# Attention weights transposed in two steps, copies of values moved forward in the queues, and a third raw buffer in the last stage

## The chip, the cores and the metric

The program runs on one core of a Trainium2 chip. The core has four engines that matter here. TensorE (PE in the profile; PEld is its loading of the stationary operand) multiplies matrices into PSUM. VectorE (DVE) and ScalarE (ACT) do element work and move results out of PSUM. SyncE (SP) issues the DMAs. Each engine works through its own queue in order and waits where an instruction needs a result of another engine. The metric is the device time of one execution in microseconds. Three runs of the kernel before took 2829.89, 2833.97 and 2838.74 us; the median is 2833.97.

## The reference, cut to what matters

Two layers work on 512 tokens of width 2048, all in float32. The first is an mLSTM with 8 heads, the second an attention over chunks with 16 heads of width 128; the attention's keys and values come from the residual stream after the first layer. Each layer normalises, modulates with a learned shift and scale, mixes, gates with SiLU, projects back, normalises again and adds to the stream.

```python
def mlstm_mixer(h, w_in, conv_w, conv_b, gate_b, g_head, w_out):
    proj = h @ w_in
    qk = silu(causal_conv(proj[..., :A_V0], conv_w, conv_b))
    v, o, z = ...                       # three more column ranges of proj
    ht = mlstm_chunkwise(q, k, v, li, lf)
    ht = rmsnorm(ht, g_head)
    y = sigmoid(o) * ht * silu(z)
    return y @ w_out

kv = hkv @ kv_w                         # keys and values, shared
qz = h @ w_in                           # queries and gate of the attention
s = einsum('blhd,bkhd->bhlk', q, k) * scale + bias
p = softmax(where(visible, s, -inf))
y = einsum('bhlk,bkhd->blhd', p, v) * silu(z)
x = x + gate * rmsnorm(y @ w_out, g_post)
```

A chunk of 64 queries sees itself and the eight chunks before it, which at 512 tokens is every earlier chunk.

## The kernel before, in words

Float32 products are made of three matmuls each: every operand is split into a high part `hi` (rounded by a copy on ACT, line 181) and a rest `lo` (a subtraction on DVE, line 182), and `mm3` adds `hi*hi`, `hi*lo` and `lo*hi` in PSUM. `split` is this pair, one ACT and one DVE instruction.

Weights come in pieces of 128 x 1024 numbers, 512 KB, in the order in which `stream()` lists them. `wpiece` (line 187) loads a piece into a `raw` buffer, may form sums of its blocks (lines 206 to 208, for products done with seven in place of eight block products, `proj_s`), and splits it into `wh` and `wl` (sums into `wsh` and `wsl`). There are two `raw` buffers (`RAW_BUFS`), and three each of `wh` and `wl`. Where `spare[0]` names a pool, every third piece (`i % 3 == 0`, line 197) takes a `raw` buffer of that pool, so that there are three.

PSUM has eight banks. Five belong to the pool `psP` and hold the products of projections (`newp`); three belong to `psA` and hold all smaller results (`newa`): scores, transposes, the attention's output.

The order of the instructions is not written out by hand. A planner takes them in the order of the program as priority and gives each engine, whenever it is free in the plan, the ready instruction of the highest priority. `tc.high_priority(AHEAD)` makes the instructions in its block count as if they stood 300 instructions earlier (`AHEAD = 300`, line 33). From the second stage on the pieces of weights are prepared under it, and so is the evacuation at the end of `proj_s`.

The stages follow each other:

- The start makes the modulation and the first products. Then eight mLSTM heads (loop at line 619). A head projects its values with `proj_b` into four banks `pv` (line 666), 128 tokens each; the last block of weights finishes the four banks one after the other. Lines 672 to 679 move the four banks to `v` tiles, three of them with `split`, the fourth with a copy. Behind that come the products of the gates: from head `HALF = 4` on `pair` and `proj_s`, which take four banks at once, named d, c, a and b (`ps_dzo`, `ps_czo`, `ps_azo`, `ps_bzo`). In head 4, `head_sums` also makes the sums of the input (`h1s`) on ACT and DVE while the values are projected.
- The output projection of the mLSTM (`rows`), then `values` (line 870): products into banks `ps_kv`, copied to SBUF by ACT at line 880 and stored. `input_sums` makes sums for the keys at the same time. The keys follow with `proj_s` (banks `ps_dk`, `ps_ck`, `ps_ak`, `ps_bk`).
- The attention (lines 973 to 1058). For head `h`, `queries` runs `proj_s` with four pieces of weights; `mid` is called ahead of the third piece. `mid` runs `mixed` for head `h-2` (weights times values into `ps_o`) and `weights` for head `h-1` (scores into `ps_s`, softmax). Behind the projection stands `flipped(h-1)`: ten 128 x 128 transposes into four tiles `ps_t`, for the blocks j = 0 to 3 with 4, 3, 2 and 1 transposes; each tile is evacuated into `pt0` to `pt3`, the first three with `split`; then `vt`, the values of the head, is split into `vv`.
- The output projection (line 1093): four groups `g` of 512 columns. Groups 0 to 2 take all four blocks of tokens at a time; group 3 takes them in two passes of two, the last with three pieces held back (`late=3`), while `finish` normalises and stores the finished rows (line 1091).

## Time and profile before

| | us |
|---|---|
| median of three runs | 2833.97 |
| the profiled execution | 2835.62 |
| its span, first to last instruction | 2833.6 |
| TensorE busy | 2788.1 |
| DVE busy | 2057.1 |
| ACT busy | 1333.3 |

The span is what the profile shows; the 2.0 us between it and the time of the same execution lie outside it. The stages in the span, read from the timeline: mLSTM heads to about 1545 us, their output projection to 1888, values and keys to 2245 (keys from 1981 to 2144), attention to 2654, the last projection to the end.

Rows of the timeline read: start, duration, engine, line, operation, `out<-in` by the program's names, shape, count, and in brackets the idle time before it with what ended it. Rows of the chain read: start, duration, what. Rows of windows give the length, then busy time (and instructions) of PE, PEld, DVE, ACT and POOL, the granted clock of TensorE as a share of full speed, the DMA engines' busy share, and GB/s. Matmuls overlap: the time one takes in a stream is the distance between starts, not its printed duration. Loads of weights appear as `wr<-in_wst`; the page gives a median of 3.5 us from issue to landing for the pieces of 512 KB.

### The profile page before, as it was taken

How to read it: one execution, taken by the hardware profiler on the slowest of the kernel's cores; microseconds unless marked ns; L12 is line 12 of the kernel's file. 1: busy time of each engine (PE TensorE's matmuls, PEld its weight loads, DVE VectorE, ACT ScalarE, POOL GpSimd, SP SyncE). 2: the span in 40 equal slices, each digit the busy share in tenths (PEclk: the TensorE clock that was granted, in tenths of full speed). 3: DMA queues.
4: the chain of work that ended last, by engine and by line, in shares of the span. 5: the costliest groups of instructions: out<-in, count | busy, mean ns of one | idle time of the engine just before them, and what ended most of it. 6: DMA issues, size and time to landing. Idle time of an engine off the chain costs nothing.

```text
span 2833.6 us, 40474 instructions
## 1 busy us (share of the span) xinstructions
PE 2788.1 (98%) x15308; PEld 2421.5 (85%) x15308; DVE 2057.1 (73%) x3488; ACT 1333.3 (47%) x1957; POOL 0.2 (0%) x4
## 2 busy tenths in 40 slices
PE   7999999999999999999999999999999999999998
PEld 5787888888888989989888888888998899999886
DVE  7986978878688776857767445567885788888525
ACT  4234524334234544544545444468434566666523
POOL 0000000000000000000000000000000000000000
PEclk9999999999999999999999999999999999999999
DMA  8875687868764232322324656788435433333624
GB/s 296 298 254 180 229 312 238 300 236 279 265 237 144 103 108 97 109 93 105 108 90 140 217 197 222 244 273 281 171 127 182 163 120 125 129 122 118 221 102 167
DMA packets 177115, 524.59 MB, mean 185 GB/s; under 512 B 18788, under 2 KB 36228, under 8 KB 176408
## 3 DMA queue, kind: packets, MB, share of 16 engines
q1 hardware_dynamic: 176920, 522.01, 54.0%
q8 instruction: 120, 1.97, 0.3%
q14 instruction: 75, 0.61, 0.1%
HBM read 488.33 MB, written 38.85 MB: 186 GB/s over the span
## 4 chain that ended last, share of the span: by engine, by line
PE 85%; DVE 7%; DMA 4%; ACT 2%; issue 2%; SPq 0%; DVEq 0%; ACTq 0%
PE ps_y L223 16%; PE ps_v L223 10%; PE ps_o L223 6%; PE ps_z L223 5%; PE ps_azo L223 4%; PE ps_qk L223 4%; PE ps_kv L223 4%; PE ps_bzo L223 3%; PE ps_l L223 3%; PE ps_az L223 3%; PE ps_cz L223 2%; PE ps_dz L223 2%; PE ps_s L223 2%; PE ps_czo L223 2%; PE ps_dzo L223 2%; DVE wl L182 2%
## 5 line engine op out<-in xcount | busy, mean ns | idle before, releaser
L181 ACT CAST wh<-wr 128x1024 fp32r<-128x1024 f32 (+3 forms) x586 | 585.0, 999 | 824.9 <-PE ps_y L223 201.5
L182 DVE TENSOR_TENSOR wl<-wr,wh 128x1024 fp32r<-128x1024 f32 (+3 forms) x586 | 678.4, 1159 | 396.2 <-ACT wh L181 395.0
L223 PE MATMUL ps_y<-wh,y 128*128 128x512 f32 x1536 | 477.4, 391 | 2.3 <-ACT wh L181 2.3
L223 PEld LDWEIGHTS ps_y<-wh,y 128*128 128x128 f32 x1536 | 288.8, 188 | 63.2 <-ACT wh L181 2.8
L223 PE MATMUL ps_v<-wh,h 128*128 128x512 f32 x1024 | 321.3, 390 | 0.0
L223 PE MATMUL ps_y<-wl,y 128*128 128x512 f32 x768 | 299.8, 390 | 0.3 <-DVE wl L182 0.3
L181 ACT CAST wsh<-ws 128x384 fp32r<-128x384 f32 (+1 forms) x205 | 129.5, 632 | 360.1 <-issue 128.9
L182 DVE TENSOR_TENSOR wsl<-ws,wsh 128x384 fp32r<-128x384 f32 (+1 forms) x205 | 144.3, 704 | 130.2 <-ACT wsh L181 129.7
L223 PEld LDWEIGHTS ps_v<-wh,h 128*128 128x128 f32 x1024 | 192.3, 188 | 39.7 <-issue 0.4
L223 PE MATMUL ps_v<-wl,h 128*128 128x512 f32 x512 | 199.8, 390 | 0.0
L381 DVE CUSTOM_DVE_ANT_0 ada<-ada,scB,cl 128x1024 f32<-128x1024 f32 x128 | 163.7, 1280 | 27.2 <-DMA ada<-in_adaT 26.9
L381 DVE CUSTOM_DVE_ANT_0 ada<-ada,scB,mod 128x1024 f32<-128x1024 f32 x128 | 163.9, 1280 | 23.7 <-DMA ada<-in_adaT 22.1
L223 PEld LDWEIGHTS ps_y<-wl,y 128*128 128x128 f32 x768 | 144.6, 188 | 30.8 <-DVE wl L182 1.1
L223 PE MATMUL ps_kv<-wh,hkv 128*128 128x512 f32 x512 | 159.4, 391 | 0.0
L206 DVE TENSOR_TENSOR ws<-wr 128x256 f32<-128x256 f32 (+1 forms) x205 | 104.8, 520 | 35.7 <-DMA wr<-in_wst 34.3
L223 PE MATMUL ps_qk<-h,wh 128*128 128x512 f32 x384 | 119.1, 390 | 0.0
L223 PE MATMUL ps_o<-h,wh 128*128 128x512 f32 x384 | 118.3, 389 | 0.0
L223 PE MATMUL ps_z<-h,wh 128*128 128x512 f32 x384 | 118.3, 389 | 0.0
L223 PEld LDWEIGHTS ps_v<-wl,h 128*128 128x128 f32 x512 | 96.2, 188 | 19.7 <-issue 0.9
L223 PEld LDWEIGHTS ps_kv<-wh,hkv 128*128 128x128 f32 x512 | 95.7, 188 | 19.6
L223 PE MATMUL ps_l<-h,wh 128*128 128x512 f32 x320 | 99.6, 393 | 1.0 <-ACT q L467 0.5
L223 PE MATMUL ps_kv<-wl,hkv 128*128 128x512 f32 x256 | 99.8, 390 | 0.0
(385 smaller groups left out, 5880.8 us busy)
## 6 DMA issues: line engine op xcount, KB each, us to landing
wr<-in_wst SPq DMA_DIRECT2D x520, 512.0 KB, 3.5
ada<-in_adaT SPq DMA_DIRECT2D x256, 512.0 KB, 5.9
xt<-nsc SPq DMA_DIRECT2D x46, 256.0 KB, 3.9
yr<-ysc SPq DMA_DIRECT2D x16, 512.0 KB, 4.4
wr<-in_wst SPq DMA_DIRECT2D x30, 256.0 KB, 4.6
wr<-in_wst SPq DMA_DIRECT2D x16, 384.0 KB, 6.0
bsc<-in_ext SPq DMA_DIRECT2D x16, 320.0 KB, 6.4
xt<-in_xT SPq DMA_DIRECT2D x4, 1024.0 KB, 6.9
```

The costliest lines, as they stand in the source:

```text
L181: nc.scalar.copy(hi, src)
L182: nc.vector.tensor_tensor(lo, src, hi.bitcast(F32), op=ALU.subtract)
L206: nc.vector.tensor_tensor(t[:, : 2 * w], r[:, w : 3 * w], r[:, : 2 * w], op=ALU.subtract)
L223: nc.tensor.matmul(ps, a, b, start=start, stop=stop)
L381: pin(nc.vector.tensor_tensor_reduce(at, at, scB[:, j * D // 2 : (j + 1) * D // 2], 1.0, mod[:, i : i + 1] if j else col(CB + i), ALU.mult ...
```

## The change

Four edits. Lines 672 to 679 move `v` out of PSUM under `high_priority(AHEAD)`, and so does the copy at line 880. In the attention, `flipped` takes the list of its blocks: blocks 0 and 1 stay behind the projection of head `h`, blocks 2 and 3 and the split of `vt` (now `split_v`) move into `turn`, which `queries` of the next head calls ahead of its second piece of weights; `mid` stays ahead of the third. In the last stage, from group 1 on, `spare[0]` is the pool `op`, so every third piece has a `raw` buffer there, 4 KB a partition more.

```diff
         for m in range(4):
-            if m < 3:
-                t = hp.tile([P, 2, S], F32R, tag="qk", name=f"v{h}_{m}", bufs=4)
-                split(t[:, 0, :], t[:, 1, :], pv[m])
-            else:
-                t = hp.tile([P, S], F32, tag="v3", name=f"v{h}_{m}")
-                nc.scalar.copy(t, pv[m])
+            with tc.high_priority(AHEAD):
+                if m < 3:
+                    t = hp.tile([P, 2, S], F32R, tag="qk", name=f"v{h}_{m}", bufs=4)
+                    split(t[:, 0, :], t[:, 1, :], pv[m])
+                else:
+                    t = hp.tile([P, S], F32, tag="v3", name=f"v{h}_{m}")
+                    nc.scalar.copy(t, pv[m])
             v.append(t)
...
-            nc.scalar.copy(v, p)
+            with tc.high_priority(AHEAD):
+                nc.scalar.copy(v, p)
...
-    def queries(h, mid):
+    def queries(h, steps):
...
-        proj_s("b_w_in", ..., kq, (2, 2), {2: mid}, True)
+        proj_s("b_w_in", ..., kq, (2, 2), steps, True)
...
-    def flipped(h, pr):
+    def flipped(h, pr, js):
         pts = []
-        for j in range(4):
+        for j in js:
...
+        return pts
+
+    def split_v(h):
         v = at.tile([P, 2, 384], F32R, tag="vv", name=f"vv{h}")
         split(v[:, 0, :], v[:, 1, :], vt[h][:, :384])
-        return pts, v
+        return v
...
     for h in range(BH + 2):
-        pr = []
+
+        def turn():
+            if h > 1:
+                pts[h - 2] += flipped(h - 2, prs.pop(h - 2), (2, 3))
+                vs[h - 2] = split_v(h - 2)
 
         def mid():
             if h > 1:
-                mixed(h - 2, *ptv.pop(h - 2), szs.pop(h - 2))
+                mixed(h - 2, pts.pop(h - 2), vs.pop(h - 2), szs.pop(h - 2))
             if 0 < h <= BH:
-                pr.extend(weights(h - 1, *qs.pop(h - 1)))
+                prs[h - 1] = weights(h - 1, *qs.pop(h - 1))
...
         if h < BH:
-            qs[h], szs[h] = queries(h, mid)
+            qs[h], szs[h] = queries(h, {1: turn, 2: mid})
         else:
+            turn()
             mid()
         if 0 < h <= BH:
-            ptv[h - 1] = flipped(h - 1, pr)
+            pts[h - 1] = flipped(h - 1, prs[h - 1], (0, 1))
...
     for g in range(4):
+        if g:
+            spare[0] = op
         gate_row(1, g)
```

More of the change, by code (lines that the diff above doesn't have):

```diff
@@ L971, in hybrid_trunk @@
     fetch_k(0)
-    def queries(h, mid):
+    def queries(h, steps):
         z = at.tile([P, 4, 256], F32, tag="z", name=f"z{h}", bufs=2)
-        proj_s("b_w_in", h2, h2s, ATT_PAIRS, z[:, 0:2, :], z[:, 2:4, :], f"z{h}", kq, (2, 2), {2: mid}, True)
+        proj_s("b_w_in", h2, h2s, ATT_PAIRS, z[:, 0:2, :], z[:, 2:4, :], f"z{h}", kq, (2, 2), steps, True)
         qz = z.rearrange("p a t -> p (a t)")
@@ L1037, in mixed @@
         nc.sync.dma_start(y2c[h // 2][:, h % 2, :], sz)
-    qs, ptv, szs = {}, {}, {}
+    qs, pts, prs, vs, szs = {}, {}, {}, {}, {}
     for h in range(BH + 2):
-        pr = []
+        def turn():
+            if h > 1:
+                pts[h - 2] += flipped(h - 2, prs.pop(h - 2), (2, 3))
+                vs[h - 2] = split_v(h - 2)
         def mid():
             if h > 1:
-                mixed(h - 2, *ptv.pop(h - 2), szs.pop(h - 2))
+                mixed(h - 2, pts.pop(h - 2), vs.pop(h - 2), szs.pop(h - 2))
             if 0 < h <= BH:
-                pr.extend(weights(h - 1, *qs.pop(h - 1)))
+                prs[h - 1] = weights(h - 1, *qs.pop(h - 1))
             if h < BH - 1:
```

## The prediction

> **What bounds the kernel now.** I read the page first (busy time, then the chain that ended last), then who TensorE waited for, then the timeline around each of those waits.

> ```profile
> span 2833.6 us, 40474 instructions
> PE 2788.1 (98%) x15308; PEld 2421.5 (85%) x15308; DVE 2057.1 (73%) x3488; ACT 1333.3 (47%) x1957; POOL 0.2 (0%) x4
> ...
> PE 85%; DVE 7%; DMA 4%; ACT 2%; issue 2%; SPq 0%; DVEq 0%; ACTq 0%
> ```

> TensorE is busy for 2788.1 of 2833.6 us and carries 85% of the chain. The change removes no matmul, so it can win only the 45.5 us in which TensorE stands still, and what a standstill costs behind it. The waits of TensorE, as far as the edits touch them:

> ```profile
> PE ps_czo L223 <- DVE v L182: 3.0, 1, 3.0
> PE ps_t L1018 <- DVE pt L182: 2.7, 5, 1.1
> PE ps_y L223 <- ACT wh L181: 2.3, 1, 2.3
> ...
> PE ps_azo L223 <- DVE v L182: 1.0, 1, 1.0
> PE ps_bk L223 <- ACT v L880: 1.0, 1, 1.0
> PE ps_ak L223 <- DVE zk L317: 1.0, 1, 1.0
> ```

> The columns are total us, times and longest. Four places: copies of `v` in one mLSTM head (3.0 + 1.0), a copy of `v` at the end of the values (1.0), the transposes of attention (2.7), the last stage (2.3). The start-up has more, but nothing there is edited.

> **Copies of v in the mLSTM heads (lines 672 to 679).** No instruction is added; the copy on ACT and the subtraction on DVE only move forward in the queues. The `ps_czo` wait occurs once, in head 4, so the other heads get nothing. There:

> ```profile
> 894.10 0.39 PE L223 MATMUL ps_v<-wh,h 128*128 128x512 f32 x1
> 894.28 0.62 ACT L181 CAST h1s<-h1r 128x512 fp32r<-128x512 f32 x1 [0.99 <-DVE h1r L328]
> 894.80 0.58 ACT L181 CAST v<-ps_v 128x512 fp32r<-128x512 f32 x1
> 897.44 0.68 DVE L182 TENSOR_TENSOR v<-ps_v,v 128x512 fp32r<-128x512 f32 x1
> 898.17 0.50 PE L223 MATMUL ps_czo<-h1s,wsh 128*128 128x256 f32 x2 [2.98 <-DVE v L182]
> 900.15 0.79 PE L223 MATMUL ps_azo<-h,wh 128*128 128x256 f32 x2 [1.00 <-DVE v L182]
> ```

> ```profile
> 521.47 43.52 PE ps_o L223 x192
> ```

> A 512-wide matmul takes 43.52/192 = 0.227 us. The last block of the value projection finishes its four banks one after the other, six matmuls each, so the first bank was complete 18 x 0.227 = 4.1 us before 894.3, at about 890.2; its copy began at 894.80, behind casts of `p`, `wh` and `h1s`. Put in front, copy and subtraction take 0.58 + 0.68 = 1.3 us behind whatever runs, so two banks are free before 895.0, where TensorE now stops, and the third about 895. That removes 2.98 + 1.00 = 4.0 us. The clock is given back too:

> ```profile
> 898.00:901.00 3.00, 1.83 (x10) 1.63 (x11) 3.00 (x7) 2.41 (x4) 0.00 (x0) 0.83 0.02 7
> 901.00:904.00 3.00, 3.00 (x11) 2.53 (x11) 2.87 (x7) 0.51 (x1) 0.00 (x0) 0.60 0.50 175
> ```

> The column before the last two is the granted clock: 0.17 x 1.83 + 0.40 x 3.0 = 1.5 us lost. Together -5.5. What is pushed back: three subtractions (2.0 us) go ahead of `h1s` and `p` work on a DVE that is busy for 3.00 of 3.00 us here. If that arrives at the weights' `wl`, 2.0 come back: -3.5 is the poor end. I take -5.5: the row below shows that the next casts of weights wait for TensorE, so they move with it.

> ```profile
> 905.62 1.05 ACT L181 CAST wh<-wr 128x1024 fp32r<-128x1024 f32 x1 [3.49 <-PE ps_bzo L223]
> ```

> [...]

> **Copies of values (line 880).** Again no new instruction.

> ```profile
> 1982.59 0.51 ACT L181 CAST wsh<-ws 128x384 fp32r<-128x384 f32 x1 [1.06 <-DVE ws L208]
> 1983.01 0.58 ACT L880 COPY v<-ps_kv 128x512 f32<-128x512 f32 x1
> ```

> ```profile
> 2001.73 0.41 DVE L314 TENSOR_TENSOR zk<-zk,ps_dk 128x256 f32<-128x256 f32 x1
> 2003.66 0.41 DVE L317 TENSOR_TENSOR zk<-zk,ps_ck 128x256 f32<-128x256 f32 x1
> ```

> The copy stood behind a `wsh` cast that waited 1.06 us on DVE. In front of it, `ps_bk` no longer waits: -1.0. But the next product stops 20 us later on `zk` of line 317, from a DVE that runs without a gap from 2001.73 to there and is not fed by this copy. TensorE would come 1.0 earlier and wait 2.0 in place of 1.0. I take 0, with ends -1.0 and +1.2 (two copies of 0.58 ahead of a `wh`).

> **Transposes in two steps (lines 1012 to 1058).** Ten transposes a head before and after, the same four evacuations, the same split of `vt`. Blocks 0 and 1 (seven transposes) stay behind the head's projection; blocks 2 and 3 (two and one) come behind the first piece of the next one, and so does the split of `vt`.

> ```profile
> 2428.35 1.14 PE L1018 MATMUL ps_t<-kcs,s 128*128 128x128 f32 x9
> 2429.25 0.48 PE L223 MATMUL ps_dz<-h2s,wh 128*128 128x256 f32 x2
> ...
> 2434.58 0.40 PE L223 MATMUL ps_dz<-h2s,wh 128*128 128x256 f32 x2
> 2434.82 0.28 PE L223 MATMUL ps_dz<-h2s,wl 128*128 128x256 f32 x1
> 2434.94 0.28 PE L223 MATMUL ps_dz<-h2s,wh 128*128 128x256 f32 x1
> 2435.29 0.30 PE L1018 MATMUL ps_t<-kcs,s 128*128 128x128 f32 x1
> ```

> ```profile
> 2434.46 1.14 DVE L182 TENSOR_TENSOR pt<-ps_t,pt 128x512 fp32r<-128x512 f32 x2
> ```

> Now nine transposes go at once into three banks, and the tenth waits for the first bank, which DVE frees at about 2435.0. From 2434.94 to 2435.29 are 0.35 us where 256-wide matmuls follow each other every 0.12 (2434.82 to 2434.94): 0.23 lost. Sixteen heads make 3.7, the five longer waits of 2.7 add some 2.3 more, the rest of them being in the 0.23: about 6.0 in all. But the tenth transpose already stands behind the first piece: 2434.58 begins the second one. After the edit it needs the same bank, freed by the same subtraction, whose inputs do not move; it should stand at the same place. And block 2 becomes a group of its own: after the nine, the first pair of matmuls took 0.48 where such a pair takes 0.40, so a third group costs 16 x 0.08 = +1.3. I take +1.0. Ends: -6.0 if the tenth's wait goes, and 16 x (0.23 + 0.08) = +5.0 if block 2 gets such a wait too. The later evacuations are covered by this room:

> ```profile
> 2411.71 0.41 DVE L182 TENSOR_TENSOR pt<-ps_t,pt 128x256 fp32r<-128x256 f32 x1
> ...
> 2414.72 0.96 DVE L182 TENSOR_TENSOR wsl<-ws,wsh 128x768 fp32r<-128x768 f32 x1 [2.40 <-ACT wsh L181]
> ```

> ```profile
> 2414.49 1.73 PE L223 MATMUL ps_o<-pt,vv 128*128 128x512 f32 x9
> ```

> `pt2` is done 2.4 us before `mixed` starts and DVE then idles for 2.4.

> [...]

> **Third raw buffer (line 1093).** From the second of four groups on, every third piece of weights is loaded into a buffer of its own, so a load waits for the piece three back and not two.

> ```profile
> 2805.83 6.61 DMA wr<-in_wst
> ...
> 2812.55 1.05 ACT wh L181
> ...
> 2813.62 1.24 DVE wl L182
> ...
> 2814.91 7.97 PE ps_y L223 x27
> ```

> ```profile
> 2814.00:2817.00 3.00, 2.70 (x8) 1.88 (x7) 1.63 (x2) 1.04 (x1) 0.00 (x0) 0.64 0.23 87
> 2817.00:2820.00 3.00, 3.00 (x12) 2.40 (x12) 0.45 (x1) 0.00 (x0) 0.00 (x0) 0.79 0.00 0
> ```

> In the last pass a piece is 12 matmuls, 2.7 us. The load issued at 2805.83 landed after 6.61 us beside the stores of finished rows; TensorE waited 2.3 for its `wh`, then lost 0.36 x 2.70 + 0.21 x 3.0 = 1.6 at the lower clock. A load issued one piece earlier, 2.7 us, covers the 2.3. I take 2.3 + 1.6 + 0.3 (the stop at 2814.91 on `wl`) = -4.2. Poor end -2.0, if the issue stays behind the stores on SP's queue.

> **Sum.** -5.5 + 0 + 1.0 - 4.2 = -8.7. The profiled execution took 2835.62 us, 2.0 outside its span; it would take 2826.9. It lies 1.65 above the median shown, 2833.97; on that scale the forecast is 2825.3, say 2825. About 0.3%, 8.5 us, is what a measurement of this kernel can tell from no change.

> **Rivals.**
> - The split does what its words say: the bank is free when blocks 2 and 3 come, and the 6.0 of waits go. For it: five of the waits are DVE being late by up to 1.1 us, which a later transpose would not see. Against it: the place of the tenth transpose, above. -5.5 - 6.0 + 1.3 - 4.2 = -14.4: 2819.5.
> - One of the two large gains fails: DVE in head 4 passes its work on to `wl` and the loads stay behind the stores, -3.5 + 1.0 - 2.0 = -4.5: 2829.5.
> - Slower: `pt2` or the split of `vt` falls behind `wsl` and `wl`. From 2414.72 that is 0.96 + 1.24 + 0.41, to 2417.3, where `mixed` wants `pt2` some 1.2 us after 2414.49. A wait of 1.5 us in 16 heads is +24, net +15: 2849. It turns the sign from 0.54 us a head (8.7/16) and means slower by 0.3% from 1.1. Against it: 2.4 us of room on both engines' rows.

> **How the numbers follow.** The forecast's case 40%, its own range 2822 to 2828, split 22 to 18 between faster and within 0.3%; the first rival 33%, faster; the second 13%, within; the slower one 14%. So faster 0.56, within 0.3% 0.30, slower 0.14. The range leaves out the slower case and little else: from 2815 (the first rival with the best ends) to 2836 (the second with block 2's +5.0).

> **What would show it.** Right: no wait of `ps_czo` or `ps_azo` on `v`, a clock of 1.00 from 898 to 904; no wait of `ps_y` on `wh` at the end; the wait of `ps_bk` gone and that of `ps_ak` longer; transposes in three groups a head, with the last still losing 0.2. Wrong: transposes two and three together without a gap; or `ps_o` waiting for `pt` or `vv` in every head.

## The result and the profile after

The changed kernel takes 2824.33 us (median of 7 runs, 2822.36 to 2826.60); the kernel before, run beside it, 2835.13 us (7 runs). The ratio is 0.9962, with a 95% interval from 0.9950 to 0.9974: 10.8 us less (7 to 14), or 0.38%: a little more than the 0.3% that can be told from no change. The forecast was 2825. The profiled execution took 2822.55 us with a span of 2820.4, so it is 1.8 us quicker than the median; 2835.62 was the one before. A difference of two single profiles, 13.1 us here, is therefore good to some 2 us.

The page of the changed kernel, its span, its engines and the shares of the chain:

```profile
span 2820.4 us, 40468 instructions
PE 2784.8 (99%) x15308; PEld 2420.6 (86%) x15308; DVE 2059.4 (73%) x3488; ACT 1332.4 (47%) x1956; POOL 0.2 (0%) x4
...
PE 86%; DVE 6%; DMA 4%; ACT 2%; issue 2%; SPq 0%; DVEq 0%; ACTq 0%
```

TensorE still has the same 15308 matmuls. It stands still for 35.6 us in place of 45.5, and its busy time falls by 3.3, about the 1.5 + 1.6 of clock in the forecast. What it waits for (total us, times, longest):

```profile
PE ps_t L1020 <- DVE pt L182: 2.5, 4, 0.9
...
PE ps_kv L223 <- DVE wl L182: 0.8, 1, 0.8
...
PE ps_ak L223 <- DVE zk L317: 0.7, 1, 0.7
...
PE ps_azo L223 <- DVE v L182: 0.5, 1, 0.5
...
PE ps_czo L223 <- DVE v L182: 0.3, 1, 0.3
```

The wait in head 4 of the mLSTM is down from 3.98 to 0.76, `ps_bk` no longer waits, `ps_y` no longer waits for weights at the end. The transposes wait as they did (2.5 after 2.7). `ps_kv` on `wl`, 0.8, is new.

Head 4 in the timeline of the changed kernel (start, duration, engine, line), and the windows behind it (the granted clock is the third number from the end):

```profile
892.18 1.22 DVE L182 TENSOR_TENSOR wl<-wr,wh 128x1024 fp32r<-128x1024 f32 x1
892.30 0.62 ACT L181 CAST h1s<-h1r 128x512 fp32r<-128x512 f32 x1 [0.96 <-DVE h1r L328]
892.82 0.58 ACT L181 CAST v<-ps_v 128x512 fp32r<-128x512 f32 x1
...
893.52 0.68 DVE L182 TENSOR_TENSOR v<-ps_v,v 128x512 fp32r<-128x512 f32 x1
...
894.26 0.50 PE L223 MATMUL ps_czo<-h1s,wsh 128*128 128x256 f32 x2 [0.26 <-DVE v L182]
```

```profile
898.00:901.00 3.00, 3.00 (x16) 2.49 (x16) 3.00 (x8) 1.13 (x4) 0.00 (x0) 1.00 0.15 40
901.00:904.00 3.00, 3.00 (x21) 2.73 (x20) 3.00 (x7) 1.58 (x3) 0.00 (x0) 1.00 0.38 141
```

The subtraction of `v` comes 0.7 us behind its cast, where it came 2.6 us behind it before (894.80 and 897.44), and the clock stays whole. The cast itself is still behind `h1s`, and the subtraction behind a `wl`: these are the 0.76 that are left. With two or four times the lead (`2 * AHEAD`, `4 * AHEAD`) the planner gives the very same order, so more precedence of this kind has nothing more to give.

The transposes of a head in attention:

```profile
2403.26 0.38 PE L1020 MATMUL ps_t<-kcs,s 128*128 128x128 f32 x2
...
2403.83 0.28 PE L223 MATMUL ps_dz<-h2s,wh 128*128 128x256 f32 x1
2404.18 0.30 PE L1020 MATMUL ps_t<-kcs,s 128*128 128x128 f32 x1
```

Three groups, of seven, two and one. The tenth starts 0.35 us behind a 256-wide matmul, as before: 0.23 lost. The last pass of the last stage:

```profile
2799.00:2802.00 3.00, 3.00 (x15) 2.50 (x14) 3.00 (x5) 1.06 (x1) 0.00 (x0) 1.00 0.90 303
2802.00:2805.00 3.00, 3.00 (x15) 2.49 (x14) 2.49 (x3) 1.05 (x1) 0.00 (x0) 1.00 0.97 371
```

TensorE is busy for all of it at a clock of 1.00, while the DMA engines are 0.90 and 0.97 busy.

### The profile page after: what moved, and what is told of

Its sections match the earlier page's. It is cut to its first block, busy times and chain, and to the rows that moved or that the text cites. A ratio compares the mean times of both kernels' runs of the same rounds, so it can differ in the third digit from the quotient of the medians.

```text
span 2820.4 us, 40468 instructions
## 1 busy us (share of the span) xinstructions
PE 2784.8 (99%) x15308; PEld 2420.6 (86%) x15308; DVE 2059.4 (73%) x3488; ACT 1332.4 (47%) x1956; POOL 0.2 (0%) x4
## 4 chain that ended last, share of the span: by engine, by line
PE 86%; DVE 6%; DMA 4%; ACT 2%; issue 2%; SPq 0%; DVEq 0%; ACTq 0%
PE ps_y L223 17%; PE ps_v L223 10%; PE ps_o L223 5%; PE ps_z L223 5%; PE ps_azo L223 4%; PE ps_qk L223 4%; PE ps_bzo L223 3%; PE ps_kv L223 3%; PE ps_az L223 3%; PE ps_l L223 3%; PE ps_cz L223 3%; PE ps_dz L223 2%; PE ps_s L223 2%; PE ps_czo L223 2%; PE ps_dzo L223 2%; PE ps_bz L223 2%
## 5 line engine op out<-in xcount | busy, mean ns | idle before, releaser
L182 DVE TENSOR_TENSOR wl<-wr,wh 128x1024 fp32r<-128x1024 f32 (+3 forms) x586 | 678.9, 1160 | 397.9 <-ACT wh L181 396.9
L181 ACT CAST wh<-wr 128x1024 fp32r<-128x1024 f32 (+3 forms) x586 | 585.6, 1000 | 802.5 <-PE ps_y L223 216.1
L223 PE MATMUL ps_y<-wh,y 128*128 128x512 f32 x1536 | 476.1, 390 | 0.0
L223 PEld LDWEIGHTS ps_y<-wh,y 128*128 128x128 f32 x1536 | 288.2, 188 | 59.8
L223 PE MATMUL ps_v<-wh,h 128*128 128x512 f32 x1024 | 322.6, 390 | 0.3 <-DVE cv L529 0.2
L223 PE MATMUL ps_y<-wl,y 128*128 128x512 f32 x768 | 299.0, 389 | 0.0
L181 ACT CAST wsh<-ws 128x384 fp32r<-128x384 f32 (+1 forms) x205 | 129.5, 632 | 356.5 <-issue 132.4
L182 DVE TENSOR_TENSOR wsl<-ws,wsh 128x384 fp32r<-128x384 f32 (+1 forms) x205 | 144.4, 704 | 125.0 <-ACT wsh L181 124.6
L223 PEld LDWEIGHTS ps_v<-wh,h 128*128 128x128 f32 x1024 | 192.3, 188 | 40.8 <-issue 1.5
L223 PE MATMUL ps_v<-wl,h 128*128 128x512 f32 x512 | 199.7, 390 | 0.0
L381 DVE CUSTOM_DVE_ANT_0 ada<-ada,scB,mod 128x1024 f32<-128x1024 f32 x128 | 163.9, 1281 | 19.8 <-DMA ada<-in_adaT 18.3
L223 PEld LDWEIGHTS ps_y<-wl,y 128*128 128x128 f32 x768 | 144.2, 188 | 29.2
L223 PE MATMUL ps_kv<-wh,hkv 128*128 128x512 f32 x512 | 159.6, 391 | 0.0
L223 PE MATMUL ps_qk<-h,wh 128*128 128x512 f32 x384 | 119.1, 390 | 0.0
L223 PE MATMUL ps_o<-h,wh 128*128 128x512 f32 x384 | 118.4, 389 | 0.0
L223 PE MATMUL ps_z<-h,wh 128*128 128x512 f32 x384 | 118.2, 389 | 0.0
L223 PEld LDWEIGHTS ps_v<-wl,h 128*128 128x128 f32 x512 | 96.1, 188 | 19.9 <-issue 0.9
L223 PEld LDWEIGHTS ps_kv<-wh,hkv 128*128 128x128 f32 x512 | 95.9, 188 | 19.6
L223 PE MATMUL ps_kv<-wl,hkv 128*128 128x512 f32 x256 | 99.8, 390 | 0.8 <-DVE wl L182 0.8
L223 PE MATMUL ps_l<-h,wh 128*128 128x512 f32 x320 | 99.2, 391 | 1.2 <-ACT oz L467 0.8
```

What stands on the lines that cost most here:

```text
L181: nc.scalar.copy(hi, src)
L182: nc.vector.tensor_tensor(lo, src, hi.bitcast(F32), op=ALU.subtract)
L223: nc.tensor.matmul(ps, a, b, start=start, stop=stop)
L381: pin(nc.vector.tensor_tensor_reduce(at, at, scB[:, j * D // 2 : (j + 1) * D // 2], 1.0, mod[:, i : i + 1] if j else col(CB + i), ALU.mult ...
```

## The experiments

The theory: each part acts in its own place, as the terms of the sum say. The main rival: the two steps of the transposes are where the gain is. The kernel before, run beside each set of experiments, took 2836.2, 2836.3 and 2836.32 us (medians of 26, 10 and 9 runs). Differences below are of medians; intervals are 95%, of the ratio on record. That ratio is not the quotient of the medians and can lie up to 0.001 from it (0.9971 against 0.9979 in the first run, 0.9998 against 1.0008 in the second), so a difference here is good to 2 or 3 us.

**One part at a time.** First the copies of `v` in the mLSTM heads alone:

```diff
-            if m < 3:
+            with tc.high_priority(AHEAD):
+                if m < 3:
...
```

> Only the copies of v in the mLSTM heads take precedence. Theory (the parts add, each in its own place): the profile of the changed kernel still shows ps_azo waiting 0.50 and ps_czo 0.26 in head 4, and the clock whole there; so 4.0 - 0.76 of wait and about 1.2 of clock go: -4.4 us against the kernel before (-5.5 as forecast, -3.5 at the poor end), a ratio near 0.9984, and no wait elsewhere grows. Rival (DVE passes its work on to the weights): -2 or less, with a wait on wl or wh behind head 4.

Measured 2830.22 us, -6.0, ratio 0.9971 (0.9960 to 0.9981). The waits of TensorE from 880 to 2144 us:

```profile
PE ps_ak L223 <- DVE zk L317: 0.6, 1, 0.6
PE ps_azo L223 <- DVE v L182: 0.5, 1, 0.5
...
PE ps_czo L223 <- DVE v L182: 0.3, 1, 0.3
```

Head 4 is as in the changed kernel. Another 1.4 us of waits are gone 1100 us later, in a stage that this edit does not touch: `ps_bk` does not wait for the copy of values, and `ps_ak` waits 0.6 in place of 1.0. The rows at that place, of the kernel before and then of this one, show what the copy no longer stands behind:

```profile
1981.66 0.69 DVE L206 TENSOR_TENSOR ws<-wr 128x512 f32<-128x512 f32 x1 [1.26 <-DMA wr<-in_wst]
```

```profile
1976.04 0.68 DVE L206 TENSOR_TENSOR ws<-wr 128x512 f32<-128x512 f32 x1
...
1977.16 0.50 ACT L181 CAST wsh<-ws 128x384 fp32r<-128x384 f32 x1
...
1977.57 0.58 ACT L881 COPY v<-ps_kv 128x512 f32<-128x512 f32 x1
```

Before, the cast of `wsh` that stands ahead of the copy waited for DVE, and DVE for a load (1.26 us). Now the load is there in time. The order of the instructions in this stage is the same on every engine, and the loads ahead of this place are issued at nearly the same distances. The wait of `ps_bk` is there in all three kernels with neither edit in force here (1.0 before, 1.2 and 0.7 in two of the runs below), and in none of the kernels with the copies of `v` in front. Why the load lands earlier in these was not tried and stays open. The profile as a whole gains nothing from it: from the first `ps_y` of the mLSTM's output projection to the first `ps_dk` of the keys it is 1.5 us longer than the one before (449.1 in place of 447.6), and from there to the attention 1.6 shorter (250.3 in place of 251.9).

Then the copies of values alone:

```diff
-            nc.scalar.copy(v, p)
+            with tc.high_priority(AHEAD):
+                nc.scalar.copy(v, p)
```

> Only the copies of values (line 880) take precedence. Theory: the wait of ps_bk (1.0) goes, and what comes behind it takes it back (in the changed kernel ps_kv waits 0.8 on wl, and ps_ak 0.7 on zk): 0, between -1.0 and +1.2, too small for a verdict; the new wait of 0.8 must show in this profile if it belongs to this edit. Rival (the 0.8 has nothing to do with these copies): no wait of ps_kv on wl, and -1.2.

Measured 2838.33 us, +2.1, ratio 0.9998 (0.9988 to 1.0008): not to be told from nothing. The waits of TensorE from 1888 to 2144 us:

```profile
PE ps_ck L223 <- DVE zk L314: 1.6, 1, 1.6
PE ps_ck L223 <- DVE wsl L182: 0.7, 1, 0.7
PE ps_ak L223 <- DVE zk L317: 0.7, 1, 0.7
```

The wait of 1.0 is gone, and the products behind it wait 3.0 in place of 1.0. The wait of `ps_kv` on `wl` is not there, so it does not come from this edit alone: the expectation that it must show was a miss. It was 0.4 in the third-buffer kernel, whose order here is that of before, and in the kernels below it comes and goes between 0 and 1.2.

Then the two steps alone (the hunks on `queries`, `flipped`, `split_v`, `turn` and `mid`):

```diff
-            qs[h], szs[h] = queries(h, mid)
+            qs[h], szs[h] = queries(h, {1: turn, 2: mid})
...
-            ptv[h - 1] = flipped(h - 1, pr)
+            pts[h - 1] = flipped(h - 1, prs[h - 1], (0, 1))
```

> Only the transposes go in two steps. Theory: the tenth transpose stands where it stood and keeps its wait in every head, and a third group of transposes costs 16 x 0.08: +1.0 us against the kernel before, ratio 1.0004, the waits of ps_t on pt about 2.5 in all as before (2.7). Rival (the split is what made the changed kernel faster): -6.0, ratio 0.998, with no wait of ps_t on pt.

Measured 2835.05 us, -1.1, ratio 0.9995 (0.9986 to 1.0004). The rival's -6.0 (0.998) lies outside. The wait that it wanted gone is there, and is even longer in this profile:

```profile
PE ps_t L1018 <- DVE pt L182: 4.1, 7, 0.9
```

Then the third raw buffer alone:

```diff
     for g in range(4):
+        if g:
+            spare[0] = op
         gate_row(1, g)
```

> Only the third raw buffer in the last stage. Theory: the wait of ps_y on wh (2.3) and the dip of the clock behind it (1.6) go, with the stops on wl around it: -4.2 as forecast, up to -5.0 by what the changed kernel shows, ratio 0.9983; granted clock 1.00 from 2814 on. Rival (loads still stand behind the stores of finished rows on SP's queue): -2.0 and a wait of ps_y on wh of about 1.

Measured 2830.24 us, -6.0, ratio 0.9974 (0.9963 to 0.9984). No wait of `ps_y` is left, and the last pass runs at full clock, beside DMA engines that are up to 0.97 busy:

```profile
2811.00:2814.00 3.00, 3.00 (x15) 2.49 (x14) 2.27 (x4) 1.07 (x2) 0.00 (x0) 1.00 0.97 372
2814.00:2817.00 3.00, 3.00 (x15) 2.32 (x13) 1.48 (x2) 0.00 (x0) 0.00 (x0) 1.00 0.31 120
```

The planner also orders the last matmuls differently with this edit, and that is worth 1.2 us. Below are the evacuation (L782) of the first of the last two blocks of tokens and the last matmul, of the kernel before and then of this one:

```profile
2821.09 0.69 DVE L782 TENSOR_TENSOR yo<-ps_y,ssum 128x512 f32<-128x512 f32 x1 [3.64 <-PE ps_y L223]
...
2822.47 0.39 PE L223 MATMUL ps_y<-wh,y 128*128 128x512 f32 x1
```

```profile
2816.52 0.69 DVE L782 TENSOR_TENSOR yo<-ps_y,ssum 128x512 f32<-128x512 f32 x1 [1.52 <-PE ps_y L223]
...
2820.17 0.39 PE L223 MATMUL ps_y<-wh,y 128*128 128x512 f32 x1
```

Behind that evacuation TensorE still has 18 matmuls of the last block to do, 4.0 us, in place of 8 in 1.8 us, so less of the first block's normalisation is left when it ends: from there to the end of the span it is 9.55 us in place of 10.77 (9.5 to 9.6 in all eight profiles with this edit, 10.8 to 10.9 in all four without it).

The four single edits add to -6.0 + 2.1 - 1.1 - 6.0 = -11.0; together they gave -10.8. That they agree so closely is partly chance: by the ratios on record the four add to -0.62%, or 17.6 us, against -0.38%. What both sums show is that two parts carry the change.

**The bank of the tenth transpose.** If it is only a bank that the tenth transpose waits for, it needs none of its own: block 3 fits into the bank of block 2.

```diff
         for j in js:
             n = S - P * j
-            ps = newa(f"ps_t{h}_{j}")
-            for i in range(j, 4):
-                nc.tensor.transpose(ps[:, P * (i - j) : P * (i - j + 1)], pr[i][:, P * j : P * (j + 1)], ident)
+            if j < 3:
+                bank = newa(f"ps_t{h}_{j}")
+                for i in range(j, 4):
+                    nc.tensor.transpose(bank[:, P * (i - j) : P * (i - j + 1)], pr[i][:, P * j : P * (j + 1)], ident)
+            if j == 2:
+                nc.tensor.transpose(bank[:, 2 * P : 3 * P], pr[3][:, 3 * P :], ident)
+            ps = bank if j < 3 else bank[:, 2 * P : 3 * P]
```

> The changed kernel, with blocks 2 and 3 of the transposes in one PSUM bank (256 + 128 of its 512 columns), so that the tenth transpose needs no bank that has to be freed. Theory (the tenth waits for a bank, and nothing else): no wait of ps_t on pt is left, groups of seven and three; 16 x (0.23 + 0.08) = 5.0, and some 1.6 of the longer waits (2.5 less 4 x 0.23), so -6.6 against the changed kernel, -17.4 against the kernel before, ratio 0.994. Rival (DVE's evacuation is what is late, and the wait only moves on to ps_o or ps_s, or to the next group of transposes): not more than -2 against the changed kernel, ratio 0.9955 or above, and a wait of about the same total elsewhere in attention.

Measured 2819.54 us, -16.8 against the kernel before, ratio 0.9941 (0.9928 to 0.9953), some 6 us less than the changed kernel's -10.8 (each against the kernel before, run beside it). No wait of `ps_t` is left, nor does another of that size take its place in attention. Busy time of TensorE in the 409 us of attention (second number), first of the changed kernel, then of this one:

```profile
2245.00:2654.00 409.00, 405.71 (x2991) 385.56 (x2990) 352.96 (x787) 263.22 (x454) 0.00 (x0) 1.00 0.40 133
```

```profile
2245.00:2654.00 409.00, 408.72 (x3023) 390.65 (x3022) 355.61 (x789) 264.14 (x455) 0.00 (x0) 1.00 0.42 135
```

The idle time falls from 3.3 to 0.3 us: what the tenth transpose waited for was a bank, and where it needs none the wait is gone.

The same without the two steps, ten transposes in one group:

```diff
-        for j in js:
+        for j in range(4):
```

> As the run before it, but the transposes are not in two steps: ten transposes in one group into three banks. Theory: one group fewer in a head than with the two steps, 16 x 0.08 = -1.3 against that run, -18.7 against the kernel before, ratio 0.9934; the two steps are worth nothing once the banks suffice. Rival (the two steps help, since ten transposes at once want three free banks at one time): a wait at the first transposes, and +2 or more against the run before it.

Measured 2821.15 us, -15.2, ratio 0.9944 (0.9932 to 0.9957): 1.6 more than the run before it, where 1.3 less was expected, and well within the intervals. Neither the first transposes nor any later ones wait for a bank. In the timelines, of seven-and-three and then of ten at once:

```profile
2403.20 0.38 PE L1021 MATMUL ps_t<-kcs,s 128*128 128x128 f32 x2
2403.42 0.27 PE L1023 MATMUL ps_t<-kcs,s 128*128 128x128 f32 x1
2403.45 0.48 PE L223 MATMUL ps_dz<-h2s,wh 128*128 128x256 f32 x2
2403.77 0.28 PE L223 MATMUL ps_dz<-h2s,wl 128*128 128x256 f32 x1
```

```profile
2399.29 1.14 PE L1021 MATMUL ps_t<-kcs,s 128*128 128x128 f32 x9
2400.27 0.27 PE L1023 MATMUL ps_t<-kcs,s 128*128 128x128 f32 x1
2400.30 0.48 PE L223 MATMUL ps_dz<-h2s,wh 128*128 128x256 f32 x2
2400.62 0.28 PE L223 MATMUL ps_dz<-h2s,wl 128*128 128x256 f32 x1
```

Nine transposes start within 0.98 us, 0.11 each. The matmul behind the last one starts 0.03 after it, 0.08 early, and the pair then takes 0.32 to the next start where such pairs take 0.24. The two cancel: a group more costs nothing.

**The two steps undone** in the changed kernel, all else kept:

```diff
-            qs[h], szs[h] = queries(h, {1: turn, 2: mid})
+            qs[h], szs[h] = queries(h, mid)
...
-            pts[h - 1] = flipped(h - 1, prs[h - 1], (0, 1))
+            ptv[h - 1] = flipped(h - 1, pr)
```

> The changed kernel with the two steps undone (the copies of v and of values and the third raw buffer stay). Theory: -1.0 against the changed kernel, -11.8 against the kernel before, ratio 0.9958, nine and one transposes with the tenth losing 0.23 in every head. Rival (the two steps gave part of the gain): +2 or more against the changed kernel, -8.5, ratio 0.997.

Measured 2828.05 us, -8.3, ratio 0.9967 (0.9955 to 0.9980). That is nearer to the rival's 0.997, but the interval holds the theory's 0.9958 too. The profile has more waits here than others with the same order:

```profile
PE ps_t L1020 <- DVE pt L182: 5.0, 7, 1.0
PE ps_t L1020 <- DVE s L1010: 1.9, 1, 1.9
```

Without the two steps that total was 2.7 and 2.7 (the kernel before, the raw buffer alone), 3.1 (copies of `v` alone), 3.7 (values alone) and 5.0; with them 2.5 and 4.1. The scatter is larger than any difference. Set against the run with ten transposes in one group, which differs from this one in the shared bank alone, the bank is worth 6.9 us (2821.15 and 2828.05), and no run of the one reaches a run of the other (up to 2822.19, from 2823.64).

**Without the edit at line 880**, on the kernel with ten transposes in one group:

```diff
-            with tc.high_priority(AHEAD):
-                nc.scalar.copy(v, p)
+            nc.scalar.copy(v, p)
```

> The run with ten transposes in one group, without the edit at line 880. Theory from the two single edits (the copies of v alone already took away the wait of ps_bk, and the copies of values alone brought waits of ps_ck): the wait of ps_kv on wl (0.8) goes and none of ps_bk on v comes, -1.1 against that run, -19.8 against the kernel before, ratio 0.993. Rival (the copy's precedence is what keeps ps_bk from waiting): a wait of ps_bk on v of about 1.0, +0.2 or more.

Measured 2817.46 us, -18.8, ratio 0.9933 (0.9921 to 0.9946). No wait of `ps_bk` on `v` comes back: with the copies of `v` in front it is absent with and without this edit, and the values' edit is not needed. Whether it costs the 1.1 us of the expectation stays open: `ps_kv` did not wait for `wl` here, but did for 1.2 us when this kernel was run again (below).

**Once more with and without the two steps**, on that best kernel, side by side:

```diff
-        for j in range(4):
+        for j in js:
```

> The best kernel so far (copies of v, third raw buffer, blocks 2 and 3 in one bank, nothing at line 880), with the transposes in two steps again, seven and three. It is set against the next run, the same without the two steps, on the same chip. By the prediction's price a group more costs 16 x 0.08: +1.3 us. By the rows since (the matmul behind a group of transposes starts 0.08 early and the next one 0.08 late) it costs nothing: within 0.5 us. By the three pairs so far, which all came out in favour of the two steps: -1.5 us.

> The best kernel so far, as the other side of the run before it: 2817.5 us or 0.9933 of the kernel before, as when it was first run; ten transposes in one group, no wait of ps_t.

Measured 2817.46 us (0.9933, 0.9921 to 0.9946) with them and 2815.49 us (0.9925, 0.9911 to 0.9938) without: +2.0. The four pairs of kernels that differ only in the two steps are -1.1, -2.5 (the changed kernel's -10.8 and the -8.3 without them), -1.6 and +2.0, a mean of -0.8; none is resolved. The best kernel, at 2815 to 2817 us some 20 us under the kernel before, has the copies of `v`, the third raw buffer and the shared bank, and neither the two steps nor the edit at line 880.

In its second run head 4 was not as quiet:

```profile
894.79 0.50 PE L223 MATMUL ps_czo<-h1s,wsh 128*128 128x256 f32 x2 [2.14 <-DVE v L182]
```

The order is the same as when that wait was 0.8. TensorE came to the gates of head 4 (`ps_dzo`) at 891.77, 1.4 us earlier than in the changed kernel, while the subtraction on DVE came 0.5 later (894.05 after 893.52). So DVE bounds this place still, and a single profile of it is good to about 1 us either way: in the four kernels that keep the order of before, the wait of `ps_czo` was 3.0, 2.3, 2.7 and 3.6.

**The same by stretches of the traces.** Inside a profile each part can be timed in its own place, from one first matmul of TensorE to another: from the `ps_dzo` of head 4 to the `ps_y` of the mLSTM's output projection (894.32 to 1531.74 before), from the `ps_dz` of attention to the `ps_y` of the last projection (2231.19 to 2634.91), and from there to the end of the span (2833.63). Lengths in us, with the number of profiles:

| stretch | part | without it | with it |
|---|---|---|---|
| head 4 to the output projection | copies of `v` | 637.1 to 639.5 (4) | 632.8 to 633.6 (7), 636.4 (1) |
| attention | shared bank | 403.7 to 406.0 (7) | 398.1 to 398.8 (5) |
| attention, no shared bank | two steps | 403.7 to 406.0 (5) | 403.7, 405.0 |
| attention, shared bank | two steps | 398.1 to 398.8 (3) | 398.4, 398.5 |
| last projection to the end | third raw buffer | 198.1 to 198.7 (4) | 191.2 to 193.7 (8) |

The 636.4 is the second run of the best kernel, just shown. Each of the three parts that count shows in its own place, and the two steps show nowhere.

## Why the prediction came out right

The time, 2824.33 against 2825.0, and the likeliest case are right. That it is right to 0.7 us is partly luck. The sum said -8.7 and -10.8 was measured; that the kernel before came out at 2835.13 beside the changed one, and not at the 2833.97 of the forecast, hides 1.2 of these 2.1. Two terms were too dear (the transposes, the third buffer) and one too good (the copies of `v`). Between the two profiles, 13.2 us of span divide into -1.2 ahead of the gates of head 4, -4.6 from there to the output projection, +0.1 from there to the attention, 0.0 in attention and -7.6 in the last stage. The first of these is in no term of the sum, and nothing here shows that an edit causes it. Two slips that change nothing: the chances add up to 0.55 and 0.31, not 0.56 and 0.30, and the outer bounds come to about 2818 and 2834 by the terms given, not 2815 and 2836. By its steps:

- **Copies of v in head 4, -5.5:** mechanism right, size a little high. 3.98 - 0.76 = 3.2 us of waits went and the 1.5 of clock: -4.7, and the stretch from head 4 on is 4.6 shorter. The step "two banks are free before 895.0, and the third about 895" failed by the two waits that are left, 0.26 and 0.50, since it put the copy behind whatever runs, while the planner still puts `h1s` and a `wl` ahead of it. DVE did not pass its work on to the weights: no wait on `wl` came behind head 4 (second rival). The edit alone timed -6.0; its profile has 4.3 of that in this stretch (637.4 to 633.1), and what the rest is stays open.
- **Copies of values, 0:** right in size, not in its course. Alone, the wait did move on, as argued, though to `ps_ck` (1.6 and 0.7) more than to `ps_ak`. In the changed kernel `ps_ak` waits 0.7, not 2.0, and `ps_bk` would not have waited without this edit either.
- **Transposes in two steps, +1.0:** right that the tenth keeps its place and its 0.23, and that the first rival's 6.0 do not come. Wrong was the term of +1.3 for a group more: the 0.48 of the first pair was read without the start ahead of it, which is 0.08 early. The row of nine transposes already said it: from 2428.35 to 2429.25 are 0.90 us for nine. What it measured is 0 in the rows, 0.0 in the stretch of attention (403.7 before and after), and -0.8, unresolved, in time.
- **Third raw buffer, -4.2:** mechanism right, size too small. Waits and clock went as said (2.3, 0.3 and 1.6), and the loads were not held up behind the stores. Alone it timed -6.0, with an interval of 4.5 to 10.5, and the last stage of its profile is 5.8 us shorter. The sum had no term for what comes behind the last matmul, and 1.2 of the 5.8 lie there.
- **Slower rival:** neither `pt2` nor the split of `vt` made `ps_o` wait.

## What to carry to other kernels

Stops of the busy engine were cured here by taking away what they waited for (a bank that need not exist, a buffer that was short), not by moving the instruction that waits: the two steps gave nothing that could be measured, one shared bank gave some 6 us and the third buffer 6.0 alone. Price a switch between kinds of matmul from start to start across the whole group, not from one longer duration. Take a wait from several profiles before it goes into a sum, time a part in its own stretch of the trace (whole runs left the worth of the two steps open, the stretch did not), and look for the effect of an edit in stages far behind it too, even where their order of instructions has not changed.

## What the hardware showed

What a stop of TensorE cost behind it was not settled by its length alone in these traces. One stop in the start-up is nearly the same in the kernel before and in the changed one (66.24 to 68.92 and 65.65 to 68.37 us: 2.7). These are windows of 3.41 us around it, of the kernel before and then of the changed one. What TensorE (second number) lacks of 3.41 is its standstill; the granted clock is the third number from the end:

```profile
63.72:67.13 3.41, 2.52 (x12) 1.72 (x10) 3.34 (x7) 0.83 (x1) 0.00 (x0) 1.00 1.04 412
67.13:70.54 3.41, 1.62 (x7) 1.34 (x8) 3.38 (x5) 0.72 (x1) 0.00 (x0) 1.00 1.01 361
70.54:73.96 3.42, 3.42 (x15) 2.25 (x13) 3.35 (x7) 1.36 (x2) 0.00 (x0) 1.00 0.98 351
```

```profile
65.80:69.21 3.41, 0.84 (x4) 0.71 (x5) 3.34 (x7) 1.15 (x2) 0.00 (x0) 1.00 1.01 375
69.21:72.62 3.41, 3.41 (x10) 2.63 (x9) 3.37 (x5) 0.85 (x2) 0.00 (x0) 0.50 0.98 361
```

```profile
336.32:339.73 3.41, 1.79 (x11) 1.27 (x10) 3.41 (x8) 2.21 (x5) 0.00 (x0) 1.00 0.95 336
339.73:343.15 3.42, 3.42 (x17) 2.83 (x16) 3.42 (x7) 1.41 (x3) 0.00 (x0) 1.00 0.98 338
```

```profile
2004.71:2008.12 3.41, 1.46 (x10) 1.26 (x11) 3.41 (x9) 1.94 (x3) 0.00 (x0) 1.00 0.58 193
2008.12:2011.53 3.41, 3.41 (x12) 2.83 (x11) 3.41 (x5) 1.38 (x2) 0.00 (x0) 0.50 0.42 167
```

From the first clock record (33 and 35 us) to the last matmul, the traces of the kernel before and of the changed one have four slots after which the clock fell, with 2.51, 2.43 and 2.45 us of standstill in the one and 2.57 in the other; in all their other slots TensorE stood still for 1.79 at most. The 1.62 and 1.95 just shown fit between these: 1.62 left the clock at 1.00, and 1.95, in two pieces, was followed by 0.50.

So two of the four parts were worth more than their waits. In the kernel before, the stops of 2.98 and 1.00 in head 4 put 2.43 us of standstill into one slot (896.57 to 899.98) and the stop in the last stage 2.45 into another (2811.45 to 2814.86); in the changed kernel the stops of both places are at most 0.76 in all. Where the slots fall differs from run to run: the stop in the start-up, 2.7 us in both traces above, lay in two slots of one and in one slot of the other, and only there was it followed by a fall.
